# A hybrid mixer, mixture-of-experts and attention kernel on Trainium2: SBUF offsets of the second block's matmul operands set to fixed residues of 256 bytes

## Chip, cores and metric

One Trainium2 chip, one NeuronCore of it. The metric is the device time of one execution of the whole program, in microseconds (us). The input is one sequence of 256 tokens of width 1024, all in fp32.

## What is computed

The reference runs a first block (layer norm, a gated delta rule and a stick-breaking attention side by side, and a mixture of 32 experts) and on its result a second block. The change is meant for the second block; cut to what matters:

```
def second_block(x, ...):                       # x: 256 tokens of width 1024
    # layer 0
    x = x + moba_attention(rms_norm_2(x), w_qkv, w_o)        # 256 tokens: one causal block, 8 heads of 128
    x = x + squared_relu_mlp(rms_norm_2(x), w_up, w_down)    # 1024 -> 4096 -> 1024
    # layer 1
    x = x + pool_mixer(rms_norm_2(x), w_groups, ls_scale)    # trailing means, four groups of 256
    x = x + squared_relu_mlp(rms_norm_2(x), w_up, w_down)
    return rms_norm_2(x)

def squared_relu_mlp(x, w_up, w_down):
    h = jax.nn.relu(x @ w_up)
    return (h * h) @ w_down
```

In the first block each token goes to the two best experts of one group. The kernel gives each expert 32 places; an expert with more tokens gets a spare block of 32, whose expert is known only at run time.

## The kernel before

**Split products.** A dense product is done in fp32r, in three matmuls. Weights and activations are each split into a high part (a ScalarE cast, line 302) and a low part (a VectorE subtraction, line 303), and high x high, low x high and high x low are summed in PSUM. `Stream` loads weights in chunks of 1 MB (line 298), two *halves* to a chunk, and splits each half into one tile `wsplit` of 128 x 2048: the high part `wh` in the first 1024 columns, the low part `wl` in the rest.

**Two forms.** `ws_half` (lines 345 to 347) holds the weights stationary and lets 256 tokens move: 24 matmuls of 256 columns for a half. `xs_half` (358 to 360) and `down` inside `mlp` (1635 to 1637) hold the activations stationary and let the weights move: 12 matmuls of 512 columns for a half. Each matmul is preceded by the load of its stationary operand (LDWEIGHTS, engine PEld in the profile), which overlaps the matmul ahead of it.

**Stages of the second block.** Its 81 chunks are, in halves: 24 of q, k and v (`xs_half`), 8 of the attention's output (`ws_half`), 64 of the first feed-forward (32 halves up by `ws_half`, 32 down by `down`), 2 of the pooling (lines 1739 to 1741, weights stationary), 64 of the second feed-forward. Steadily, four halves up alternate with four halves down.

**Where the operands lie.** The second block's split tiles come from two pools in turn, `cvt` and `cvt2`, two tiles each; the pool changes after every two halves, shifted by one:

```
pool, tag = self.extra.get(self.i - 1) or (cvp[self.i // 2 % len(cvp)], "cv")
w = pool.tile([128, 2048], F32R, tag=tag, name="wsplit")
```

so that of four halves in a row the first and the fourth lie in one pool and the two between in the other. In the built program the tiles of `cvt` begin on a multiple of 256 bytes of a partition, those of `cvt2`, some 110 KB further on, 96 bytes past one (called *offset 0* and *offset 96* below; only the remainder by 256 is meant). The activations begin at offset 0 (`xh`, `xl`), 64 (`mhh`, `mhl`, the squared ReLU's two parts) or 96 (`oh`, `ol` of the attention; `ph`, `plo` of the pooling). Rows inside these tiles are multiples of 256 bytes apart. The offsets 64 and 96 come from small tiles that are allocated ahead: `r2` (8 bytes), `rss` (16), `rst`.

**Order.** A scheduler puts each engine's instructions in order when the program is built. In the experts' stage DVE (VectorE) does, besides its share of the products, two small chains. The *rotation* (lines 1164 to 1189, tiles `pos`, `ang`, `ki`, `kf`) makes angles for the second block's attention. *Who is next* (`who_is_next`, lines 1198 to 1209, tiles `xact`, `xjk`, `xwho`, `xwhoi`) finds the expert of the first spare block; SP reads `xwhoi` into registers (`where`, lines 1213 and 1214) to issue the three loads of that expert's weights (`spare_weights`, line 1219), and behind those, in SP's order, stand the other loads of experts' weights (line 922). `spare_tokens` (1230 to 1245) gathers the block's tokens (`xG`, `xGc`).

Of the kernel before, what the change touches and what calls it, by code (L numbers as in the profile page):

```python
# [10 lines left out]
F32 = mybir.dt.float32  # L11
F32R = mybir.dt.float32r
I32 = mybir.dt.int32
# [42 lines left out]
# --------------------------------------------------------------------------  # L56
# constants that depend on shapes alone, packed by column
# --------------------------------------------------------------------------
# [53 lines left out]
def _pool_matrix():  # L112
    """the trailing mean less the token itself, by window: [t', 144 of the first t | 128 of the last t]"""
    t = np.arange(SEQ)
    m = np.zeros((128, 4, 272), np.float32)
    for g, w in enumerate(WINDOWS):
        cnt = np.minimum(t + 1, w).astype(np.float32)
        inside = (t[:, None] <= t[None, :]) & (t[:, None] > t[None, :] - w)
        f = np.where(inside, np.float32(1.0) / cnt[None, :], 0.0) - np.eye(SEQ)
        m[:, g, :144] = f[:128, :144]  # L120
        m[:, g, 144:] = f[128:, 128:]
    return np.ascontiguousarray(m.reshape(128, 1088))


# order of the half chunks of the first stream of weights
# [3 lines left out]
def _fill_order():  # L129
    """dense work that fills the gaps of the recurrent mixers"""  # L130
    o = []
    sb = [[("sb", 3 * j + i) for i in range(3)] for j in range(4)]
    zs = [("z", i) for i in range(4)]
    g = [("g", m) for m in range(8, 16)] + [("g", m) for m in range(LATE, 8)]
    for c in FILL_SPEC:
        o += sb[int(c)] if c in "0123" else [zs.pop(0)] if c == "z" else [g.pop(0)]
    o += zs + g
    return o
# [4 lines left out]
             + [("o", i) for i in range(8)])  # L143

# [112 lines left out]
# --------------------------------------------------------------------------  # L257
# the kernel
# --------------------------------------------------------------------------
# [3 lines left out]
def tile_hybrid_block(ctx: ExitStack, tc: tile.TileContext, A, out, dump=None, stop=99):  # L263
# [41 lines left out]
    class Stream:  # L305
        """a dense part's weights in the order of their use, each split into two parts of 12 bits"""

        def __init__(self, dram, n_chunks, g_halves=(), extra={}):
            self.g_halves, self.extra, self.depth = g_halves, extra, 2
            self.dram, self.i, self.n, self.raw, self.q, self.got = dram, 0, n_chunks, [], [], 0  # L310
# [6 lines left out]
        def split(self):  # L317
            i, q = divmod(self.i, 2)
            self.i += 1
            if q == 0:  # L320
                self.load(i + N_RING)
                self.cur = self.raw.pop(0)
            s = slice(q * 1024, q * 1024 + 1024)
            pool, tag = self.extra.get(self.i - 1) or (cvp[self.i // 2 % len(cvp)], "cv")
            w = pool.tile([128, 2048], F32R, tag=tag, name="wsplit")
            wh, wl = w[:, :1024], w[:, 1024:]
            split_into(wh, wl, self.cur[:, s], G if self.i - 1 in self.g_halves else V)
            self.q.append((wh, wl))
# [9 lines left out]
    def ws_half(stream, m0, nk, xh, xl, width, fn, newbank):  # L338
        """out[m, t] for the m tiles of half a chunk: weights stationary, tokens moving; fn(m, psum)"""
        wh, wl = stream.half()  # L340
        for q in range(8 // nk):
            p = newbank()
            for k in range(nk):
                o = (q * nk + k) * 128
                PE.matmul(p[:, :width], wh[:, o:o + 128], xh[:, k, :], start=k == 0, stop=False)  # L345
                PE.matmul(p[:, :width], wl[:, o:o + 128], xh[:, k, :], start=False, stop=False)  # L346
                PE.matmul(p[:, :width], wh[:, o:o + 128], xl[:, k, :], start=False, stop=k == nk - 1)  # L347
            fn(m0 + q, p)

    def xs_half(stream, k0, nk, xh, xl, banks, t0=0):  # L350
        """out[t, 512] over two k tiles: tokens stationary, weights moving"""
# [10 lines left out]
    # 1 / sqrt(x): a first guess from the bits, two steps of rising order  # L362
# [21 lines left out]
    def rsqrt1(x):  # L384
        """of one column"""
# [13 lines left out]
    def moments(mv, s):  # L399
        """mean and variance of the rows, in one piece or two"""  # L400
# [8 lines left out]
    def ln_stats(s, eps=1e-5):  # L409
        """mean and 1 / deviation of the rows"""  # L410
# [27 lines left out]
    def warm(n):  # L438
        """matmuls whose result nobody wants: the tensor engine's clock stays up over a wait"""
# [34 lines left out]
    # rows of tokens, normalised; their gain and bias come with the transposing  # L474
# [20 lines left out]
    # a/b columns  # L495
# [4 lines left out]
    # delta-net channels: projection, causal convolution (of half weights: u), silu = u (1 + tanh u)  # L500
# [37 lines left out]
    def invert(At, n, levels, nm):  # L538
        """transposed inverse of I + A from A transposed, by doubling the size of the inverted blocks"""
# [35 lines left out]
    # the stick-breaking heads' work lies where the first of the experts' weights come  # L575
# [9 lines left out]
    def delta():  # L585
        # token scalars by head: beta, decay, exp(decay), exp(last decay - decay)
# [17 lines left out]
        # rows of k, their norms; back  # L604
# [86 lines left out]
        # what waits for q  # L691
# [18 lines left out]
        # and for v  # L710
# [22 lines left out]
        # states and outputs, chunk by chunk  # L733
# [14 lines left out]
        for c in range(2):  # L748
# [35 lines left out]
            # rms norm over the head, of the output scaled by q's norm  # L784
# [97 lines left out]
    def router_weights():  # L882
        """the router on rows less their mean: weights times the norm's gain less their mean; the bias's share"""
# [25 lines left out]
    def prefetch(n):  # L909
        """expert chunks on their way: up to n"""  # L910
# [58 lines left out]
    # first weights of the experts, while the dense part goes on  # L969
# [3 lines left out]
    # the delta-net's gates, its branch, merge; the gates' sigmoid is (1 + tanh) / 2  # L973
# [79 lines left out]
    # group: softmax, first maximum (of the probabilities: exp(d) is 1 from d = -2^-25 on)  # L1053
# [13 lines left out]
    # the two best experts of the group  # L1067
# [14 lines left out]
    # place of each token in the queue of its expert  # L1082
# [6 lines left out]
    def one_hot(g):  # L1089
        """[token, expert of four and place]"""  # L1090
# [7 lines left out]
    # weights of the two experts  # L1098
# [16 lines left out]
    # experts with more tokens than places: further blocks of CAP tokens, numbered over the experts  # L1115
# [21 lines left out]
    prefetch(n_slots)  # L1137

    def gather(g, Gt):
        """the tokens of four experts, transposed; the norm's gain and bias on the way"""  # L1140
# [13 lines left out]
    # the first gathering goes on between the first products  # L1154
# [5 lines left out]
    # rotation: angles reduced to [-pi, pi]  # L1160
# [17 lines left out]
    ki = moe.tile([128, 32], I32, name="ki")  # L1178
    kf = moe.tile([128, 32], F32, name="kf")
# [15 lines left out]
    def who_is_next():  # L1195
        """the expert whose block has the number in ctr, its group and place there (0, 0 and no tokens past the last)"""
        act = rt([32], "xact")
# [5 lines left out]
        jk = rt([32], "xjk")  # L1203
# [17 lines left out]
    def spare_tokens(act, off):  # L1221
        """the block's tokens, transposed, and its combining rows"""
# [4 lines left out]
        jk = rt([32], "xjk")  # L1227
# [22 lines left out]
    def spare_block(xx, pm, weights):  # L1250
        """an expert's output for the block; weights(i): two k tiles of gate and up, then two of down by half"""
# [36 lines left out]
    # the first of these blocks goes with the rest, any more in a loop  # L1288
# [24 lines left out]
    for g in range(NG):  # L1313
# [71 lines left out]
        if g == NG - 2:  # L1385
            # the residual's rows, with the first norm's gain and bias: they join the sums of the experts' outputs
# [26 lines left out]
    post = ctx.enter_context(tc.tile_pool(name="post", bufs=1, reuse_waits="tile"))  # L1413
    cvp.append(ctx.enter_context(tc.tile_pool(name="cvt2", bufs=2, reuse_waits="tile")))
    wpost = Stream(A["wpost"], 81, G_POST)

    def scaled(x, k, gname, xh, xl):
        """a k tile times the norm's gain, in two parts"""
# [21 lines left out]
    def mean_square(x, m, acc):  # L1440
        """sums of squares of the k tiles m - 1 and m, over those before"""
# [11 lines left out]
    def total(acc):  # L1453
        """one tile of sums from two of two"""
# [6 lines left out]
    def rstd(s):  # L1461
        """of sums of squares by token along the partitions: [128, 2]"""
# [11 lines left out]
    def to_rows():  # L1474
        """x with the tokens along the partitions"""
# [115 lines left out]
    def residual(gname, xh, xl, acc):  # L1591
        """adds a product to the residual; the next norm's operand and sum of squares follow"""
# [19 lines left out]
    def mlp(xh, xl, acc, n_last, after):  # L1612
# [3 lines left out]
        r2 = post.tile([128, 2], F32, tag="r2", name="r2")  # L1616
# [22 lines left out]
        def scale():  # L1639
            """1 / mean square, by token along the partitions"""  # L1640
# [34 lines left out]
    def rstd_rows(c, ss):  # L1675
        """of the rows' mean squares by half"""
        t = post.tile([128, 1], F32, tag="rst", name="rst")
# [10 lines left out]
    ss = post.tile([128, 2, 2], F32, tag="rss", name="rss")  # L1688
# [61 lines left out]
    ss = post.tile([128, 2, 2], F32, tag="rss", name="rss")  # L1750
# [38 lines left out]
```

## Time and profile before

| | us |
|---|---|
| runs: median of 3 (lowest, highest) | 1030.16 (1026.87, 1032.97) |
| the profiled execution: span from first to last instruction | 1031.7 |
| PE (matmul) busy | 957.0 |
| DVE, ACT busy | 588.1, 444.6 |

The profiled execution's own time outside its span is not given; the span is 1.5 us above the median of the runs and inside their range. PE is TensorE's matmuls, PEld its weight loads, DVE VectorE, ACT ScalarE, POOL GpSimd, SPq the DMA issues of SyncE. A matmul's duration holds its passage through the array, so matmuls that follow each other overlap in the rows: what one costs in a dense stretch is the distance from its start to the next one's start. The windows of single halves below have their edges at the start of the first matmul of each half, as the timeline shows these starts.

### The profile page before, as it was taken

To read this page: it belongs to the slowest core of one execution; us is meant where nothing else is said; L and a number is where in the kernel's file an instruction comes from. 1 tells how busy PE (TensorE), PEld (TensorE's weight loads), DVE (VectorE), ACT (ScalarE), POOL (GpSimd) and SP (SyncE) were. 2 spreads that over 40 slices of the span, in tenths; PEclk is the share of its full clock that TensorE was granted. 3 is DMA by queue.
4 is the path that set the end of the run, shared out by engine and by line. 5 is a ranking of instruction groups with operands and counts; after the bars stand their busy time and mean duration, and the time that the engine had idled before them with its cause. 6 is when DMAs were issued, how large, how long until landed. Compare 5 with 4: busy or idle time off the path is not lost.

```text
span 1031.7 us, 15809 instructions
## 1 busy us (share of the span) xinstructions
PE 957.0 (93%) x6369; PEld 778.3 (75%) x6369; DVE 588.1 (57%) x1131; ACT 444.6 (43%) x774; POOL 104.8 (10%) x75
## 2 busy tenths in 40 slices
PE   4889999999999988869979999999999999999996
PEld 3788988899884523324358889989999789999885
DVE  8887657584763211102276777655555586555554
ACT  3554655454432111102065565544444564444442
POOL 5343333000300000000040001000000020000001
PEclk9889999999999999989999999999999999999998
DMA  9222212749779999989956435455555525555521
GB/s 369 105 98 87 102 44 83 264 160 355 302 307 390 415 426 422 426 362 426 382 185 222 164 123 186 164 186 182 185 182 186 182 87 200 186 182 179 190 82 41
DMA packets 34234, 227.37 MB, mean 220 GB/s; under 512 B 3936, under 2 KB 4704, under 8 KB 7664
## 3 DMA queue, kind: packets, MB, share of 16 engines
q1 hardware_dynamic: 34160, 226.36, 57.8%
q8 instruction: 50, 0.82, 0.3%
q14 instruction: 24, 0.20, 0.1%
HBM read 225.29 MB, written 1.05 MB: 219 GB/s over the span
## 4 chain that ended last, share of the span: by engine, by line
PE 74%; DVE 10%; DMA 7%; ACT 4%; POOL 2%; issue 2%; SPq 0%; ACTq 0%; POOLq 0%; DVEq 0%
PE bank L347 10%; PE bank L346 9%; PE bank L345 9%; DMA wexp<-in_wexp_dram 6%; PE acc L1635 6%; PE acc L1636 6%; PE acc L1637 6%; PE bank L1335 5%; PE bank L359 3%; PE bank L360 2%; PE bank L358 2%; PE bank L1376 2%; PE acc L1303 2%; PE bank L1147 2%; DMA wraw<-in_wpre_dram 2%; DVE wsplit L303 2%
## 5 line engine op out<-in xcount | busy, mean ns | idle before, releaser
L303 DVE TENSOR_TENSOR wsplit<-wraw,wsplit 128x1024 fp32r<-128x1024 f32 x212 | 269.0, 1269 | 159.8 <-ACT wsplit L302 158.0
L302 ACT CAST wsplit<-wraw 128x1024 fp32r<-128x1024 f32 x222 | 231.7, 1045 | 152.5 <-PE acc L1637 94.9
L347 PE MATMUL bank<-xl,wsplit 128*128 128x256 f32 x512 | 144.3, 282 | 3.4 <-DVE xl L1420 3.4
L346 PE MATMUL bank<-xh,wsplit 128*128 128x256 f32 x512 | 143.9, 281 | 0.0
L345 PE MATMUL bank<-xh,wsplit 128*128 128x256 f32 x512 | 143.7, 281 | 0.0
L1635 PE MATMUL acc<-wsplit,mhh 128*128 128x512 f32 x256 | 101.7, 398 | 0.0
L1636 PE MATMUL acc<-wsplit,mhh 128*128 128x512 f32 x256 | 101.2, 395 | 0.0
L1637 PE MATMUL acc<-wsplit,mhl 128*128 128x512 f32 x256 | 101.1, 395 | 0.0
L347 PEld LDWEIGHTS bank<-xl,wsplit 128*128 128x128 f32 x512 | 97.2, 190 | 4.2 <-DVE xl L1420 4.2
L345 PE MATMUL bank<-hh,wsplit 128*128 128x256 f32 (+1 forms) x320 | 97.1, 303 | 1.6 <-DVE rcb L891 1.5
L347 PE MATMUL bank<-hl,wsplit 128*128 128x256 f32 (+1 forms) x320 | 94.3, 297 | 4.2 <-DVE hl L303 4.2
L345 PEld LDWEIGHTS bank<-xh,wsplit 128*128 128x128 f32 x512 | 97.1, 190 | 0.6
L346 PEld LDWEIGHTS bank<-xh,wsplit 128*128 128x128 f32 x512 | 97.0, 190 | 0.5
L346 PE MATMUL bank<-hh,wsplit 128*128 128x256 f32 (+1 forms) x320 | 94.8, 296 | 0.0
L1335 PE MATMUL bank<-wexp,xt 128*32 128x512 f32 x512 | 65.0, 622 | 7.4 <-DMA wexp<-in_wexp_dram 7.4
L347 PEld LDWEIGHTS bank<-hl,wsplit 128*128 128x128 f32 x320 | 63.4, 199 | 5.1 <-DVE hl L303 5.1
L345 PEld LDWEIGHTS bank<-hh,wsplit 128*128 128x128 f32 x320 | 64.0, 200 | 2.6 <-DVE rcb L891 1.7
L346 PEld LDWEIGHTS bank<-hh,wsplit 128*128 128x128 f32 x320 | 63.9, 200 | 0.3 <-issue 0.2
L1625 ACT ACTIVATE relu<-bank 128x256 f32<-128x256 f32 x64 | 24.7, 385 | 87.1 <-PE bank L347 87.1
L1637 PEld LDWEIGHTS acc<-wsplit,mhl 128*128 128x128 f32 x256 | 48.0, 188 | 11.5
L1636 PEld LDWEIGHTS acc<-wsplit,mhh 128*128 128x128 f32 x256 | 48.1, 188 | 11.2 <-DVE wsplit L303 0.3
L1635 PEld LDWEIGHTS acc<-wsplit,mhh 128*128 128x128 f32 x256 | 48.1, 188 | 11.0
(506 smaller groups left out, 1633.4 us busy)
## 6 DMA issues: line engine op xcount, KB each, us to landing
wexp<-in_wexp_dram SPq DMA_DIRECT2D x99, 1024.0 KB, 19.2
wraw<-in_wpost_dram SPq DMA_DIRECT2D x81, 1024.0 KB, 4.7
wraw<-in_wpre_dram SPq DMA_DIRECT2D x30, 1024.0 KB, 4.8
h<-in_x_dram SPq DMA_DIRECT2D x2, 512.0 KB, 4.1
eb<-in_rowv_dram SPq DMA_DIRECT2D x2, 512.0 KB, 10.1
out_dram<-of SPq DMA_DIRECT2D x4, 256.0 KB, 2.2
cpre<-in_cst_dram SPq DMA_DIRECT2D x1, 915.5 KB, 10.3
pmat<-in_poolm_dram SPq DMA_DIRECT2D x1, 544.0 KB, 4.5
```

The lines of the kernel that those rows point to most:

```text
L302: S.copy(hi, src)
L303: (sub or V).tensor_tensor(lo, src, hi.bitcast(F32), op=OP.subtract)
L345: PE.matmul(p[:, :width], wh[:, o:o + 128], xh[:, k, :], start=k == 0, stop=False)
L346: PE.matmul(p[:, :width], wl[:, o:o + 128], xh[:, k, :], start=False, stop=False)
L347: PE.matmul(p[:, :width], wh[:, o:o + 128], xl[:, k, :], start=False, stop=k == nk - 1)
L358: PE.matmul(banks[c], xh[:, k, tsl], w1, start=k == 0, stop=False)
L359: PE.matmul(banks[c], xh[:, k, tsl], w2, start=False, stop=False)
L1335: PE.matmul(pg[32 * e:32 * e + 32, :], xt[:, k, 32 * e:32 * e + 32], w[:, e, :], start=k == 0, stop=k == 7)
L1625: S.activation(t, p[:, :SEQ], AF.Relu)
L1635: PE.matmul(ac[c][n], hh_, wh, start=g == 0 and k == 0, stop=False)
L1636: PE.matmul(ac[c][n], hh_, wl, start=False, stop=False)
L1637: PE.matmul(ac[c][n], hl_, wh, start=False, stop=g == 7 and k == 3)
```

## The change

Besides dropping comments, docstrings and blank lines, it does three things.

```
+UP = [j < 2 or (j < 30 and (j - 2) % 4 < 2) for j in range(32)]
+STILL = [False] * 24 + [True] * 8 + [u for u in UP for _ in range(2)] + [True] * 2 + [u for u in UP for _ in range(2)]
+SHIFT = 24
...
-        def __init__(self, dram, n_chunks, g_halves=(), extra={}):
-            self.g_halves, self.extra, self.depth = g_halves, extra, 2
+        def __init__(self, dram, n_chunks, g_halves=(), extra={}, still=()):
+            self.g_halves, self.extra, self.depth, self.still = g_halves, extra, 2, still
...
-            w = pool.tile([128, 2048], F32R, tag=tag, name="wsplit")
-            wh, wl = w[:, :1024], w[:, 1024:]
+            if self.still:
+                o = SHIFT if self.still[self.i - 1] else 0
+                w = pool.tile([128, 2048 + 64], F32R, tag=tag, name="wsplit")
+                wh, wl = w[:, o:o + 1024], w[:, o + 1024:o + 2048]
+            else:
+                w = pool.tile([128, 2048], F32R, tag=tag, name="wsplit")
+                wh, wl = w[:, :1024], w[:, 1024:]
...
-    wpost = Stream(A["wpost"], 81, G_POST)
+    wpost = Stream(A["wpost"], 81, G_POST, still=STILL)
```

`STILL` says of each of the second block's 162 halves whether its weights are stationary. If so, its two parts begin 24 floats (96 bytes) into a tile that is 256 bytes longer. The first block's stream is as it was.

```
-        r2 = post.tile([128, 2], F32, tag="r2", name="r2")
+        r2 = post.tile([128, 64], F32, tag="r2", name="r2")[:, :2]
...
-        t = post.tile([128, 1], F32, tag="rst", name="rst")
+        t = post.tile([128, 64], F32, tag="rst", name="rst")[:, :1]
...
-    ss = post.tile([128, 2, 2], F32, tag="rss", name="rss")
+    ss = post.tile([128, 2, 32], F32, tag="rss", name="rss")[:, :, :2]
```

These small tiles now fill 256 bytes each. In the built program every `wsplit` tile and all of `xh`, `xl`, `mhh`, `mhl`, `oh`, `ol`, `ph`, `plo` begin at offset 0. So in the second block stationary weights lie at offset 96 against moving activations at 0, and moving weights at offset 0 against stationary activations at 0.

```
-    ki = moe.tile([128, 32], I32, name="ki")
-    kf = moe.tile([128, 32], F32, name="kf")
+    ki = moe.tile([128, 32], I32, tag="xjk", name="ki")
+    kf = moe.tile([128, 32], F32, tag="xact", name="kf")
...
-        act = rt([32], "xact")
+        act = rt([32], "xact", tag="xact")
...
-        jk = rt([32], "xjk")
+        jk = rt([32], "xjk", tag="xjk")
```

The rotation's `kf` and `ki` now share their memory with `xact` and `xjk`.

**What it moves.** ACT, POOL and SP keep their order; DVE and PE change at one place, in the experts' stage. On DVE, before, who is next and both `xG` stand right after the counting of blocks (`xsv` is of the same helper, `G` and `hid` belong to the experts):

```order
L1198 TENSOR_SCALAR xact<-cx,ctr 128x32
L1201 TENSOR_SCALAR xoff<-cx,ctr 128x32
L1199 SCALAR_TENSOR_TENSOR xact<-ci,ctr,xact 128x32
...
L1209 CAST xwhoi<-xwho 1x2
L1230 SCALAR_TENSOR_TENSOR xjk,xs_3548<-xact,xsv 128x32
L1231 SCALAR_TENSOR_TENSOR xjk,xs_3548<-xact,cmb 128x32
L1232 TENSOR_SCALAR xG<-cst,xs_3548 128x32
...
L1051 TENSOR_TENSOR G<-cst,rk 128x256
L1361 TENSOR_TENSOR hid<-hid,bank 128x256
```

In the changed kernel (its line numbers are 10 higher) they stand behind the whole rotation, whose last rows are the two of `ang`:

```order
L1197 TENSOR_TENSOR ang<-ang,kf 128x32
L1199 TENSOR_SCALAR ang<-ang 128x64
L1208 TENSOR_SCALAR xact<-cx,ctr 128x32
L1209 SCALAR_TENSOR_TENSOR xact<-ci,ctr,xact 128x32
L1216 SCALAR_TENSOR_TENSOR xjk,xwho<-xact,cst 128x32
L1284 TENSOR_SCALAR ctr<-ctr 128x1
L1216 SCALAR_TENSOR_TENSOR xjk,xwho<-xact,cst 128x32
L1219 CAST xwhoi<-xwho 1x2
...
L1242 TENSOR_SCALAR xG<-cst,xs_3548 128x32
...
L1391 COPY ys<-bank 128x256
L1242 TENSOR_SCALAR xG<-cst,xs_3548 128x32
```

So all of the rotation, and the experts' `G`, `hid`, `xt`, `hT` and `ys` rows that stood between the two chains, now come ahead of `xwhoi`. On PE, at the same place, before and then in the changed kernel:

```order
L1376 MATMUL bank<-wexp,hT 32x512 x12
L1237 MATMUL bank<-xG,h_77 128x32 x3
L1376 MATMUL bank<-wexp,hT 32x512 x4
L1237 MATMUL bank<-xG,h_77 128x32 x13
L1245 MATMUL bank<-cst,xGc 32x128 x2
```

```order
L1386 MATMUL bank<-wexp,hT 32x512 x12
L1247 MATMUL bank<-xG,h_77 128x32
L1255 MATMUL bank<-cst,xGc 32x128
L1386 MATMUL bank<-wexp,hT 32x512 x4
L1247 MATMUL bank<-xG,h_77 128x32 x15
L1255 MATMUL bank<-cst,xGc 32x128
```

One transpose of `xGc` moved ahead of an expert's four matmuls and two gathering matmuls moved behind them; the rest is in the order of before.

## Rows read from the trace of the kernel before

**Rows 1.** The page: busy time by engine, and the last chain's shares by engine.

```profile
PE 957.0 (93%) x6369; PEld 778.3 (75%) x6369; DVE 588.1 (57%) x1131; ACT 444.6 (43%) x774; POOL 104.8 (10%) x75
...
PE 74%; DVE 10%; DMA 7%; ACT 4%; POOL 2%; issue 2%; SPq 0%; ACTq 0%; POOLq 0%; DVEq 0%
```

**Rows 2.** Windows by stage: length, then busy of PE, PEld, DVE, ACT, POOL; clock, DMA, GB/s.

```profile
309.00:345.00 36.00, 34.12 (x274) 16.24 (x270) 14.68 (x70) 8.29 (x18) 0.00 (x0) 1.00 0.96 392
345.00:509.00 164.00, 140.99 (x890) 57.73 (x890) 26.22 (x64) 18.56 (x47) 0.00 (x0) 0.97 0.98 408
520.00:1032.00 512.00, 492.75 (x3089) 441.06 (x3088) 326.10 (x556) 260.34 (x426) 25.26 (x18) 0.99 0.47 162
```

**Rows 3.** Waits of PE in the second block: total, times, longest.

```profile
PE bank L1430 <- DVE r L396: 3.7, 1, 3.7
PE bank L347 <- DVE xl L1420: 3.4, 4, 1.3
```

**Rows 4.** Windows of single halves, PE only: four up, then two down.

```profile
673.49:676.37 2.88, 2.88 (x26) 1.00 0.35 148
676.37:679.18 2.81, 2.81 (x26) 1.00 0.75 236
679.18:682.00 2.82, 2.82 (x26) 1.00 0.34 142
682.00:684.87 2.87, 2.87 (x26) 1.00 0.60 188
...
690.92:693.72 2.80, 2.80 (x13) 1.00 0.32 135
693.72:696.51 2.79, 2.79 (x13) 1.00 0.72 235
```

**Rows 5.** The same for two halves of the attention's output, split tiles of `cvt2`.

```profile
629.20:632.08 2.88, 2.88 (x27) 1.00 0.79 242
632.08:634.95 2.87, 2.87 (x26) 1.00 0.30 123
```

**Rows 6.** The same for halves of q, k, v: tiles of `cvt` thrice, then of `cvt2`.

```profile
553.88:556.60 2.72, 2.72 (x14) 1.00 0.01 3
...
563.08:565.84 2.76, 2.76 (x13) 1.00 0.90 306
565.84:568.56 2.72, 2.72 (x13) 1.00 0.18 75
568.56:571.37 2.81, 2.81 (x13) 1.00 0.40 87
```

**Rows 7.** Groups by line in 673.49 to 696.51: DVE's and ACT's share of a split.

```profile
L303 DVE TENSOR_TENSOR wsplit<-wraw,wsplit 128x1024 fp32r<-128x1024 f32 x8 | 9.8, 1226 | 8.1 <-ACT wsplit L302 8.1
...
L302 ACT CAST wsplit<-wraw 128x1024 fp32r<-128x1024 f32 x8 | 8.4, 1045 | 6.3 <-PE acc L1637 6.3
```

**Rows 8.** Timeline of DVE around who is next and the rotation's end: start, duration.

```profile
312.56 0.23 DVE L1198 TENSOR_SCALAR xact<-cx,ctr 128x32 f32<-128x32 f32 x1
...
313.67 0.16 DVE L1209 CAST xwhoi<-xwho 1x2 int32<-1x2 f32 x1
...
342.68 0.20 DVE L1189 TENSOR_SCALAR ang<-ang 128x64 f32<-128x64 f32 x1
```

**Rows 9.** SP's read of `xwhoi`: duration ns least, median, most; first and last start.

```profile
L1213 SPq TENSOR_LOAD <-xwhoi x1: 483/483/483, 329.0 to 329.0; - x1
```

**Rows 10.** Timeline of SP's loads: start, time from first to last, count.

```profile
328.61 0.33 SPq L922 DMA_DIRECT2D wexp<-in_wexp_dram  x1
331.16 14.37 SPq L1219 DMA_DIRECT2D wexp<-in_wexp_dram  x3
345.63 6.07 SPq L922 DMA_DIRECT2D wexp<-in_wexp_dram  x6
```

**Rows 11.** Line 922's load of 328.6: us from issue to landing.

```profile
DMA to landing us min/median/max: 20.1/20.1/20.1
```

**Rows 12.** A window as in rows 2.

```profile
346.00:351.00 5.00, 5.00 (x39) 3.71 (x32) 1.50 (x4) 0.37 (x1) 0.00 (x0) 1.00 1.03 390
```

More of the change, by code (lines that the diff above doesn't have):

```diff
@@ L1226, in spare_tokens @@
         s1 = rt([2, 2], "xs1")
-        jk = rt([32], "xjk")
+        jk = rt([32], "xjk", tag="xjk")
         for c in range(2):
@@ L1749, in tile_hybrid_block @@
     nf = row("norm_final", act1, "rowsA")
-    ss = post.tile([128, 2, 2], F32, tag="rss", name="rss")
+    ss = post.tile([128, 2, 32], F32, tag="rss", name="rss")[:, :, :2]
     fin = ctx.enter_context(tc.tile_pool(name="fin", bufs=1, reuse_waits="tile"))
```

## The prediction

> **What bounds the kernel now.** I read the page first: PE is busy for 957 of 1031.7 us and holds 74% of the last chain [rows 1]. That is a mean over stages, so the windows by stage come next [rows 2]. From 309 to 509 us the DMA engines are busy for 96 to 98% of the time: there the loads of the experts' weights set the end. From 520 us to the end, the second block, DMA is at 47%, DVE at 326 of 512 us, and PE at 493 of 512. PE's waits there are few, the two largest 3.7 and 3.4 us in all [rows 3]. So in the second block a shorter matmul is a shorter kernel, as long as nothing behind PE becomes late.
>
> A matmul's price can't be read from its duration, since neighbours overlap; it is read from the length of a half in which PE never stops. Four halves up in a row take 2.88, 2.81, 2.82 and 2.87 us [rows 4]. They do the same work on the same activations, at a granted clock of 1.00 in each. What differs is the pool: the first and the fourth have weights at offset 0, the two between at 96, and the activations are at 0. DMA load doesn't sort them: of the slow ones one has a DMA share of 0.35 and one of 0.60, of the fast ones one 0.75 and one 0.34. So (weights 0, activations 0) costs 2.875 and (96, 0) 2.815 us.
>
> That it is the pair of offsets, and not the pool, the attention's output says: there the weights lie in the pool that was fast above, but the activations are at 96 too, and the halves take 2.88 and 2.87 us [rows 5].
>
> With the weights moving, q, k and v tell the pools apart the other way round: weights at 0 against stationary activations at 0 take 2.72 to 2.76 us, weights at 96 take 2.81 [rows 6]. The halves down take 2.80 and 2.79 in one pool and in the other [rows 4]: there the stationary activations are at 64 in both.
>
> **The change, part by part.** It adds no instruction to the second block and removes none; it moves every half to the better pair of its form.
>
> *Up, 64 halves.* 32 of them are at (0, 0) and go to (96, 0): 32 x (2.875 - 2.815) = 1.9 us.
>
> *Down, 64 halves.* They go from stationary 64, moving 0 or 96, to 0 and 0. No half down shows that pair, but q, k and v have the same form and shape. Their steady value is 2.72; 2.76 stands directly behind other work. I take 2.73, near the steady value since all halves down will be alike: 64 x (2.795 - 2.73) = 4.2 us. The bounds: 64 x (2.795 - 2.76) = 2.2 us and 64 x (2.795 - 2.72) = 4.8 us; if the pair is not the cause here, nothing.
>
> *q, k, v, 24 halves.* 12 have their weights at 96: 12 x (2.81 - 2.73) = 0.9 us, between 0.4 (if half of it vanishes in the interruptions by the attention's heads) and 1.1.
>
> *Attention's output, 8 halves,* from (0, 96) or (96, 96) to (96, 0): 8 x (2.875 - 2.815) = 0.5 us. *Pooling, 2 halves,* of the same form: 0.1 us.
>
> *What hides the splits.* ACT takes 1.05 us and DVE then 1.23 us to split a half [rows 7], 2.28 us in a row if nothing overlaps. A half down will take 2.73, so the split stays hidden, with some 0.4 us to spare. Half of the splits in these rows already write to offset 96, the tiles of `cvt2`, so writing there can't be much dearer. The longer tiles and the small tiles of 256 bytes cost space and no time.
>
> *The experts' stage.* Here something gets later. `kf` now owns the memory of `xact`, so who is next can start only when the rotation is through. Before, it ran from 312.56 to 313.83, 1.27 us; the rotation ended at 342.88 [rows 8]. So `xwhoi` is ready at 342.88 + 1.27 = 344.15. SP read it at 329.0 [rows 9] without waiting and issued the first spare load 2.16 us later [rows 10]. Now SP stands still for 15.1 us, and the load goes out at 344.15 + 2.16 = 346.3 instead of 331.2. Behind it in SP's order stand the other two spare loads and all later loads of experts' weights. In a stage bounded by DMA that could cost up to 15.1 us. What covers it is the queue: the load ahead, issued at 328.6, needed 20.1 us to land [rows 11], at 348.7, because those ahead of it came first. At 392 to 408 GB/s [rows 2] a load of 1 MB takes about 2.6 us, so the engines still have more than 2 us of work when the first spare load comes. The third spare load was held until 345.6 anyway [rows 10], so that line 922 goes on at about 348 instead of 345.6, and behind it the order is as before. The window from 346 to 351 with its DMA share of 1.03 [rows 12] stays full. I count 0; the bounds are 0 and 2 us, the latter if a new load needs that long to get the engines going. On PE the one transpose that moved waits for `xGc` some tenths of a us, in a stage where PE waits for weights later.
>
> **Sum.** 1.9 + 4.2 + 0.9 + 0.5 + 0.1 = 7.6 us less, all in the second block. Against the profiled span: 1031.7 - 7.6 = 1024.1. The median of the runs shown is 1.5 us below that span, so for the median: 1030.2 - 7.6 = 1022.6 us.
>
> **Rivals.**
> 1. *Halves down don't care.* Their activations come fresh from ACT and DVE and their sums alternate between four banks; if that sets 2.80 and not the 64, only the rest remains: 1.9 + 0.9 + 0.5 + 0.1 = 3.4, so 1026.8 us. For it: no row shows a half down at another offset. Against it: 2.80 is also what q, k, v cost at a bad pair [rows 6], and at 64 the pool makes no difference, as if one bad operand were enough.
> 2. *Offsets decide nothing.* The two pools also lie some 110 KB apart in a partition, and the place could be what a read feels; the change leaves the places and the turns of the pools as they are, so the halves stay as they are: 1030.2 us. Against it: the same pool is fast in rows 4 and slow in rows 5. The Trainium skill speaks for this rival: by "TensorE: Matmul & The Clock Gate", section "Step-by-step: what each phase is for", TensorE has two independent read ports to SBUF, and loading the next weights takes nothing from the running matmul, so where the two operands lie would not matter and the time would be that of before. The trace disagrees: 2.88 against 2.81 us for equal halves [rows 4].
> 3. *Slower: SP's wait reaches the DMA engines.* The place is line 1213. If the queue's 20 us do not cover it (the spare loads come in small pieces, and three at once behind an empty queue may start slowly), the stall enters in full: 1030.2 + 15.1 - 7.6 = 1037.7 us. It begins to cost when the first spare load leaves later than about 346.5, and each us beyond that costs one; the gain is eaten at 354. For it: SP stands behind one word. Against it: 328.6 + 20.1 is later than 346.3 [rows 10, 11].
>
> **How the numbers follow.** A measurement of this kernel can tell about 0.5% from no change, 5.2 us. My forecast has a chance of 0.71, the first rival 0.14, the second 0.09, the third 0.06. The forecast's own bounds: at least 1.9 + 2.2 + 0.4 + 0.5 = 5.0 us, at most 1.9 + 4.8 + 1.1 + 0.6 = 8.4, so 1021.8 to 1025.2; the runs' scatter of 3 us to either side of their median adds to it. The range reaches over the first rival, from 1019.5 to 1027.2. Faster by over 0.5%: the forecast but for its lowest end, 0.67. Within 0.5%: that end and the first two rivals, 0.27. Slower: the third, 0.06.
>
> **What would show it right or wrong.** Halves up all 2.81 to 2.82 us, halves down 2.72 to 2.76, the attention's output 2.82, q, k, v 2.72 to 2.76, each at a clock of 1.00. The matmuls' mean durations hardly move; the distances between their starts do. SP's read of `xwhoi` starts late or lasts to about 344, the first spare load leaves near 346, and the DMA share from 346 to 351 stays at 1. The second block should begin where it did. I am wrong if halves down stay at 2.80, if halves of one form still come in two lengths, if new waits of PE for `wsplit` appear, or if the stage of the experts ends later.

## The result, and the profile after

The changed kernel took 1025.93 us in the median of 22 runs (1019.52 to 1029.30), the kernel before, run beside it, 1031.11 (1026.87 to 1034.81). The ratio is 0.9943, with an interval of 0.9928 to 0.9958: by the ratio 5.9 us less, between 4.3 and 7.4. The forecast was 1022.6, 7.6 less than a median of 1030.16. The profiled run took 1027.14 us, 2.3 of them outside its span of 1024.8.

The page of the changed kernel, busy time and the last chain's shares, beside [rows 1]:

```profile
PE 945.8 (92%) x6369; PEld 773.4 (75%) x6369; DVE 589.4 (58%) x1131; ACT 444.5 (43%) x774; POOL 104.5 (10%) x75
...
PE 77%; DVE 12%; ACT 4%; POOL 2%; DMA 2%; issue 2%; SPq 0%; ACTq 0%; POOLq 0%; DVEq 0%
```

PE is busy for 11.2 us less with the same number of matmuls, and no other engine's time moved by more than 5. Windows of single halves, columns as in [rows 4 to 6]; first four halves up and two down, then two of the attention's output, then three of q, k, v:

```profile
672.34:675.15 2.81, 2.81 (x25) 1.00 0.46 192
675.15:677.97 2.82, 2.82 (x26) 1.00 0.76 221
677.97:680.78 2.81, 2.81 (x26) 1.00 0.36 152
680.78:683.60 2.82, 2.82 (x26) 1.00 0.61 186
686.79:689.51 2.72, 2.72 (x14) 1.00 0.80 241
689.51:692.23 2.72, 2.72 (x14) 1.00 0.35 145
617.41:620.22 2.81, 2.81 (x26) 1.00 0.00 0
620.22:623.04 2.82, 2.82 (x26) 1.00 0.00 0
563.26:565.98 2.72, 2.72 (x13) 1.00 0.87 280
565.98:568.70 2.72, 2.72 (x13) 1.00 0.25 105
568.70:571.43 2.73, 2.73 (x14) 1.00 0.43 90
```

In this profile every form now has one length, apart from halves beside a wait or other work, where before it had two or more: up 2.81 to 2.82, down 2.72, q, k, v 2.72 to 2.73. The second block's two largest waits of PE are those of [rows 3], so nothing took the place of what went:

```profile
PE bank L1440 <- DVE r L406: 3.7, 1, 3.7
PE bank L357 <- DVE xl L1430: 3.4, 4, 1.3
```

The experts' stage is the other half of the story. DVE's timeline: the rotation's last instruction, then the cast into `xwhoi`, beside [rows 8] (start, duration):

```profile
341.92 0.20 DVE L1199 TENSOR_SCALAR ang<-ang 128x64 f32<-128x64 f32 x1
...
343.05 0.16 DVE L1219 CAST xwhoi<-xwho 1x2 int32<-1x2 f32 x1
```

SP's read of `xwhoi` (beside [rows 9]), then SP's issues (beside [rows 10]), then how long the three spare loads took to land (beside [rows 11]):

```profile
L1223 SPq TENSOR_LOAD <-xwhoi x1: 470/470/470, 343.2 to 343.2; - x1
```

```profile
344.95 2.07 SPq L1229 DMA_DIRECT2D wexp<-in_wexp_dram  x3
347.12 1.98 SPq L932 DMA_DIRECT2D wexp<-in_wexp_dram  x1
```

```profile
DMA to landing us min/median/max: 7.8/9.5/11.4
```

Windows of 1 us around it (length, clock, DMA share, GB/s), where [rows 12] had 1.03 and 390:

```profile
346.00:347.00 1.00, 1.00 0.69 125
347.00:348.00 1.00, 1.00 0.94 350
348.00:349.00 1.00, 1.00 1.03 391
```

The first spare load left at 344.95, 1.4 us earlier than forecast. All the same the engines ran dry: 125 GB/s for one us where they had moved 390.

For all runs I took the same few moments from the traces' records: when the load ahead of the first spare load landed, when that spare load was issued and landed, how long from the load ahead to the last of the experts' loads, and how long the second block took from the start of its fourth half to the end of the last instruction that an engine computes. (us; zero is the first such instruction, 0.3 us off the profile's zero.)

```
run            ahead    spare    spare    landed   to last  second
               landed   issued   landed   apart    load     block
before         348.44   330.91   351.06   2.62     160.0    490.9
after          347.00   344.69   352.47   5.47     162.9    483.0
again          346.76   343.62   349.53   2.77     160.8    483.2
offsets_only   339.61   321.91   342.23   2.62     160.3    483.1
move_only      338.89   336.27   341.91   3.02     161.4    489.9
sweep_weights  347.72   344.87   350.55   2.82     161.2    488.3
sweep_acts     348.10   344.44   352.08   3.98     162.7    488.7
sweep_fine     349.93   346.25   353.07   3.14     162.1    484.8
all_at_64      344.56   327.04   347.20   2.64     160.0    482.5
no_padding     348.33   330.96   350.97   2.64     160.1    487.8
kick_scan      342.63   325.25   345.26   2.63     159.9    478.1
at_224         339.07   321.58   341.69   2.62     160.2    481.5
kick_rows      346.54   329.15   349.18   2.64     160.4    480.9
kick_at_96     348.08   330.34   350.72   2.64     160.2    484.3
```

In the changed kernel the second block is 7.9 us shorter and the experts' stage 2.9 longer. The difference of the spans, 6.9, is these two, 1.4 us that the stages ahead happened to be faster, and 0.5 between the last load and the second block.

### The profile page after: what moved, and what is told of

It is laid out like the page before. It is cut to its first block, busy times and chain, and to the rows that moved or that the text cites. A ratio compares the mean times of both kernels' runs of the same rounds, so it can differ in the third digit from the quotient of the medians.

```text
span 1024.8 us, 15811 instructions
## 1 busy us (share of the span) xinstructions
PE 945.8 (92%) x6369; PEld 773.4 (75%) x6369; DVE 589.4 (58%) x1131; ACT 444.5 (43%) x774; POOL 104.5 (10%) x75
## 4 chain that ended last, share of the span: by engine, by line
PE 77%; DVE 12%; ACT 4%; POOL 2%; DMA 2%; issue 2%; SPq 0%; ACTq 0%; POOLq 0%; DVEq 0%
PE bank L357 10%; PE bank L356 9%; PE bank L355 9%; PE bank L1345 6%; PE acc L1645 5%; PE acc L1646 5%; PE acc L1647 5%; PE bank L1157 3%; PE bank L1386 3%; PE acc L1313 3%; PE bank L369 2%; PE bank L370 2%; PE bank L368 2%; DMA wexp<-in_wexp_dram 2%; DVE wsplit L308 2%
## 5 line engine op out<-in xcount | busy, mean ns | idle before, releaser
L1645 PE MATMUL acc<-wsplit,mhh 128*128 128x512 f32 x256 | 100.4, 393 | 0.0
L1646 PE MATMUL acc<-wsplit,mhh 128*128 128x512 f32 x256 | 99.8, 390 | 0.0
L1647 PEld LDWEIGHTS acc<-wsplit,mhl 128*128 128x128 f32 x256 | 48.1, 188 | 10.1
```

Source lines behind the costliest of these rows:

```text
L1645: PE.matmul(ac[c][n], hh_, wh, start=g == 0 and k == 0, stop=False)
L1646: PE.matmul(ac[c][n], hh_, wl, start=False, stop=False)
L1647: PE.matmul(ac[c][n], hl_, wh, start=False, stop=g == 7 and k == 3)
```

## Experiments

### The same kernel again, and the two halves of the change apart

`again` is the changed kernel. `offsets_only` keeps its offsets and shares `kf` and `ki` with tiles of the spare block that are written later, so that every engine has the order of before (the sharing saves room in SBUF; no run shows how much would be lacking without it). `move_only` is the kernel before with the change's sharing alone.

```
 offsets_only, against the changed kernel
-    ki = moe.tile([128, 32], I32, tag="xjk", name="ki")
-    kf = moe.tile([128, 32], F32, tag="xact", name="kf")
+    ki = moe.tile([128, 32], I32, tag="xhT", name="ki")
+    kf = moe.tile([128, 32], F32, tag="xx", name="kf")
...
-        act = rt([32], "xact", tag="xact")
+        act = rt([32], "xact")
...
-        xx = rt([8, CAP], "xx")
+        xx = rt([8, CAP], "xx", tag="xx")
```

> The changed kernel once more, beside the next two. First theory: the offsets take some 7.3 us from the second block and the moved who-is-next gives 1.5 to 3 us back in the experts' stage, in sum 0.994 of the kernel before. Rival: the offsets take 5.9 us and the move nothing: the same 0.994. This run only sets the mark for the other two on the same chip.

> The offsets as in the changed kernel, but ki and kf share memory with xhT and xx instead of xjk and xact, which brings every engine back to the order of before. First theory: SP reads xwhoi without waiting, the landing of the first spare load follows the one ahead after 2.5 us instead of 5.5, and the kernel is 1.5 to 3 us faster than the changed one: about 7.3 us less than before, a ratio of 0.993 or a little under. Rival: the same time as the changed kernel, 0.994 to 0.9945, since the stage waits elsewhere anyway.

> The kernel before with only the shared memory of ki and kf, no offset changed. First theory: SP waits at line 1213 to about 344, the first spare load lands 5.5 us behind the one ahead, and the kernel is 1.5 to 3 us slower than before: 1.0015 to 1.003. Rival: the queue covers it and the time is that of before, 1.000.

Measured: `again` 0.9925 (0.9902 to 0.9948), `offsets_only` 0.9911 (0.9890 to 0.9932), `move_only` 1.0005 (0.9980 to 1.0029). By time alone `again` and `offsets_only` can't be told apart; the traces can. The offsets are worth 7.8 us in the second block (490.9 to 483.1) with no instruction moved. The moved who is next gains nothing and costs 0.8, 1.4 and 2.9 us in the experts' stage in three traces, for one and the same order; the time of `move_only` alone, between 2.1 us less and 3.0 more than before, is too coarse to show such a cost. So the offsets are the whole gain, and this way of sharing is a price that the change need not have paid.

### Which offsets matter, and to whom

`sweep_weights` gives the split weights 0, 32, ... 224 bytes in turn, two halves each, counted apart for the two forms; `sweep_fine` does so in steps of 16 where they are stationary and leaves 0 where they move; `sweep_acts` leaves the weights at 0 and moves the activations of down, 32 bytes further with each group.

```
-                o = SHIFT if self.still[self.i - 1] else 0
+                o = self.offset(self.i - 1)
...
+        def offset(self, i):
+            same = [j for j in range(i) if self.still[j] == self.still[i]]
+            return 8 * (len(same) // 2 % 8)
```

```
+            oa = 8 * g
+            hh_ = post.tile([128, 4 * SEQ + 64], F32R, tag="mh", name="mhh", bufs=2)[:, oa:oa + 4 * SEQ].rearrange("p (m t) -> p m t", t=SEQ)
```

> The changed kernel with the split weights' offset stepped through 0, 32, 64 ... 224 bytes, two halves each, apart for halves whose weights are stationary and whose weights move; activations stay at 0. Read is the length of each half. First theory, the pair decides: with stationary weights 2.88 us at 0 and 2.82 at 96, and some other offsets that are as good; with moving weights 2.72 at 0 and 2.80 or more at most others. Rival, place or pool decides: all halves of a form alike, or two lengths that follow the pools' turns and not the offset.

> The changed kernel with the squared ReLU's parts, stationary in the halves down, moved to 0, 32, 64 ... 224 bytes, one offset for each group of four halves; the weights stay at 0. First theory, the pair of offsets decides: 2.72 us a half at 0, about 2.80 at 64 as before the change, most others 2.79 to 2.81. Rival (halves down do not care about their stationary operand; the gain came from the weights that no longer lie at 96): 2.72 at every offset.

> The changed kernel with stationary weights at 0, 16, 32 ... 240 bytes, two halves each, activations and moving weights at 0. The coarse sweep gave halves up of 2.88 at 0 and 160, 2.84 at 32, 2.82 at 96 and 192 and, at 64, 2.83 in the first feed-forward but 2.72 to 2.74 in the second. First theory, offset alone: each offset has one length, the same in both feed-forwards, and 64 was disturbed by its neighbours of other offsets; a smooth course between the points of the coarse sweep. Rival, a second condition (the bank of PSUM, or how the two reads fall in step): 48 to 80 again have two lengths, by feed-forward.

Each was executed once (1031.93, 1033.33 and 1029.66 us), for the lengths of the halves. Halves down in `sweep_acts`, weights at 0, stationary activations at 0, 32 and 192:

```profile
669.52:672.24 2.72, 2.72 (x13) 1.00 0.35 145
692.26:695.06 2.80, 2.80 (x14) 1.00 0.30 126
803.34:806.09 2.75, 2.75 (x14) 1.00 0.63 179
```

Lengths by offset, worked out from the starts in the traces (us; a dash where only halves beside a wait lay there, a plus where the shortest of four stands and the longest took 0.02 to 0.04 more):

```
bytes past a multiple of 256       0     32    64    96    128   160   192   224
down, weights move, acts at 0      2.72  2.80  2.75  2.80  2.79  2.81  2.80  2.80
down, acts move,  weights at 0     2.72  2.80  2.80  2.81  2.80  2.80  2.75  2.80
up, first feed-forward (fine)      2.88  2.84  -     2.85  2.88  2.88  2.83  2.80
up, second feed-forward (fine)     2.87  2.84  2.83  2.82  2.88  2.88  2.83  2.80
up, second feed-forward (steps 32) 2.88  2.84  2.72+ 2.82  2.85+ 2.88  2.83  2.80+
```

For down the answer is plain: both operands on a multiple of 256 is the one pair that gives 2.72, and moving either of them costs 0.03 to 0.09 us. For up the picture has a flaw: at 64, with the same remainders, the table holds 2.83 and 2.72. `sweep_acts` shows the same at 96, where all its halves up lie. A half of the group behind halves down with activations at 0, then one of the group behind halves down with activations at 32:

```profile
677.78:680.60 2.82, 2.82 (x27) 1.00 0.70 232
700.70:703.55 2.85, 2.85 (x26) 1.00 0.78 230
```

Behind halves down at 0, 64, 128 and 160 the halves up took 2.82 us, behind those at 32 and 96 they took 2.85, in both feed-forwards alike.

### 64 instead of 96, and the small tiles as they were

`all_at_64` is `offsets_only` with SHIFT = 16. `no_padding` is `offsets_only` with `r2`, `rst` and `rss` as small as before, so that down's activations lie at 64 and the attention's at 96 again, and the second pool's weights at 96 more than the first's.

```
-SHIFT = 24
+SHIFT = 16
```

```
-        r2 = post.tile([128, 64], F32, tag="r2", name="r2")[:, :2]
+        r2 = post.tile([128, 2], F32, tag="r2", name="r2")
```

> The offsets of the changed kernel but stationary weights at 64 instead of 96, and the order of before (ki and kf share with xhT and xx). If 64 by itself is the cheapest, as in the second feed-forward of the sweep: halves up of 2.72 us, 74 x 0.095 = 7 us less than the same with 96, a ratio of 0.984 to 0.985. If only the second feed-forward gains: half of that, 0.988. If the short halves were an effect of mixed offsets: 2.83, that is 1 us more than with 96, 0.992.

> The shift of stationary weights stays, the order is that of before, but r2, rst and rss are as small as they were: activations go back to 64 and 96, the second pool back to 96, so that half of the moving weights lie at 96 and half of the stationary ones at 192. First theory: halves up 2.82 at 96 and 2.83 at 192; halves down 2.79 to 2.81 as before the change, q, k, v of the second pool 2.81; in sum some 5.5 us more than with the padding, a ratio of 0.997. Rival (halves down do not care): 0.993.

`no_padding` gave 0.9977 (0.9949 to 1.0004): down back at 2.79 to 2.80 us, a second block of 487.8. So some 4.7 of the 7.8 us hang on the small tiles, the part of the diff that looks like a trifle. `all_at_64` gave 0.9925 (0.9893 to 0.9958), and a puzzle. Three of its halves up, the first before any half down, the others behind halves down:

```profile
649.68:652.40 2.72, 2.72 (x26) 1.00 0.59 244
666.50:669.32 2.82, 2.82 (x25) 1.00 0.43 180
669.32:672.15 2.83, 2.83 (x27) 1.00 0.74 243
```

In both feed-forwards eight halves up stand ahead of the first down; the last six of them, which ran without a wait, took 2.72, and all that came behind halves down 2.83, although the four tiles in turn have the very same addresses in both. So neither remainder nor place can be all; what ran just before is the likely difference.

### A small matmul between a half down and a half up

`kick_scan` puts one small matmul of the same operands, overwritten by the next, ahead of each group of four halves up that follows halves down, with another width in each of the 12 groups.

```
+            if kick:
+                PE.matmul(p[:, :kick], wh[:, :128], xh[:, 0, :kick], start=True, stop=True)
             for k in range(nk):
```

> The kernel with stationary weights at offset 64 and the order of before, with one small matmul more ahead of each group of four halves up that follows halves down (12 groups; its columns 16, 32, 64, 96, 128, 192 in the first feed-forward and 48, 80, 112, 160, 224, 256 in the second). Without it, halves up at the very same addresses took 2.72 us in the first six of a feed-forward and 2.827 in all that follow halves down. Theory A (two rhythms): loads and matmuls settle into one of two steps to each other, and stay in it until something disturbs them; then some widths of the small matmul bring the four halves behind it to 2.72 us and others leave them at 2.827, four alike each time. Theory B (the company decides: once halves down run between, the sums, splits and ReLUs of ACT and DVE that run beside the halves up are others): all 48 halves stay at 2.827, whatever the width. The time is one look: by A, with half of the widths good, some 2.5 us less than the 1021.3 of that kernel, and 12 small matmuls of some 0.1 us more, so about 1020; by B about 1022.5.

One execution, 1015.25 us (before: 1029.55, median of 11); what it is read for is the lengths inside it. A group with a small matmul of 16 columns in front, all four halves, then two halves of the last group, whose small matmul has 256 columns:

```profile
664.23:667.08 2.85, 2.85 (x26) 1.00 0.47 195
667.08:669.80 2.72, 2.72 (x26) 1.00 0.69 235
669.80:672.52 2.72, 2.72 (x26) 1.00 0.37 151
672.52:675.25 2.73, 2.73 (x27) 1.00 0.56 168
...
974.08:976.90 2.82, 2.82 (x26) 1.00 0.02 6
976.90:979.73 2.83, 2.83 (x26) 1.00 0.00 0
```

Eleven widths of twelve, from 16 to 224 columns, bring the halves to 2.72, the first with the small matmul's own time on top; only 256, which is one more matmul of the usual width, leaves them at 2.83. The small matmul costs 0.13 to 0.15 us and gains four times 0.107. The second block is 4.4 us shorter than in `all_at_64`. That the company of other engines decides (theory B) is out: nothing was changed there, and 44 of the 48 halves changed their length.

### Two more versions, and the kick at 96

`at_224` has the halves up at 224 and the attention's output and pooling at 64. `kick_rows` has 64 everywhere and uses, for four of the six groups, the transposes of the residual's rows as the disturbance, by calling `next(rows)` ahead of `up(g + 1)`; the other two groups get a small matmul. `kick_at_96` is `offsets_only` with a small matmul of 96 columns in all 12 groups.

```
-SHIFT = 24
+SHIFT = [16 if 24 <= i < 32 or 96 <= i < 98 else 56 for i in range(162)]
```

```
+            if 0 < g < 5:
+                t = next(rows)
             if g < 7:
                 up(g + 1)
             if g == 0:
                 scale()
-            if 0 < g < 5:
-                t = next(rows)
```

> The order of before, activations at offset 0, weights at 0 where moving; stationary weights at 224 in the halves up (2.80 us in the finest sweep, in both feed-forwards) and at 64 in the attention's output and the pooling (2.72 to 2.83 us where they lay there). Against the kernel with 96 everywhere, whose halves up took 2.815: 64 x 0.015 = 1.0 us, six of them that took 2.847 another 0.3, and the attention's output 7 x 0.127 = 0.9: 2.2 us less. Expected, if a length goes with its offset: halves up 2.80, the second block about 481 us, ratio to the kernel before about 0.989. If the length depends on the rhythm that was carried in from the half before: some halves up above 2.82 although all lie at 224, ratio 0.991 or more.

> Stationary weights at offset 64, the order of before in the experts' stage. Of each feed-forward's six groups of halves up that follow halves down, four now come directly behind the four transposes of the residual's rows (which stood ahead of the next halves down until now), and the last two behind a small matmul of 96 columns. Theory A (two rhythms, 2.72 and 2.827 us for a half up at the same addresses, kept until something comes between): any other matmul between a half down and a half up puts the rhythm right, the transposes too. Then all halves up take 2.72: 12 groups x 4 x 0.107 = 5.1 us less than with 64 and no kick, 4 small matmuls cost 4 x 0.12 = 0.5, and 8 halves down that no longer follow transposes save 0.1 each: 5.4 us less, a second block of 477 instead of 482.5 us, a ratio to the kernel before of about 0.987. Rival (only a matmul of the same operands puts it right): the 8 groups behind transposes stay at 2.827 us, 1.2 us less at most, ratio 0.991.

> The order of before, stationary weights at offset 96 as in the change, and a small matmul of 96 columns more ahead of each of the 12 groups of halves up that follow halves down. Without it, halves up at 96 took 2.847 us in the first six of the second feed-forward, and 2.815 behind halves down. Theory A (each offset has two rhythms, and what came just before chooses): the small matmul sends the 48 halves up behind it to the other rhythm, 2.847: here the kick is a loss of 48 x 0.03 = 1.4 us and 12 x 0.12 = 1.4 more for itself, a second block of 483.1 + 2.9 = 486. Rival (the kick just clears something, and any half up behind it is faster): 2.72 to 2.80 us, a second block of 481 or less.

`at_224`: 0.9916 (0.9889 to 0.9943), its second block 481.5. Halves up behind halves down took 2.80 as expected, but the first six of each feed-forward 2.83: this offset too has two lengths, the other way round from 64.

`kick_rows`: 0.9874 (0.9840 to 0.9907), the best ratio measured with an interval; the second block took 480.9, not 477. Three halves of the first group behind transposes, then three of the third:

```profile
670.36:673.18 2.82, 2.82 (x27) 1.00 0.30 122
673.18:675.90 2.72, 2.72 (x26) 1.00 0.83 268
675.90:678.62 2.72, 2.72 (x26) 1.00 0.28 117
714.87:717.78 2.91, 2.91 (x27) 1.00 0.27 110
717.78:720.61 2.83, 2.83 (x27) 1.00 0.94 313
720.61:723.43 2.82, 2.82 (x26) 1.00 0.15 61
```

Six of the eight groups behind transposes went to 2.72, the third of each feed-forward stayed at 2.83, and this time the attention's output and the first six halves up ran at 2.83 as well, at the addresses at which they had taken 2.72 in `all_at_64`. Those 19 halves and two groups make up 2.9 of the 3.9 us that were missed, the eight first halves behind transposes, 2.82 to 2.91 long, another 0.8.

`kick_at_96`: one execution, 1027.21 us. The halves behind the kick kept their 2.815:

```profile
671.59:674.51 2.92, 2.92 (x26) 1.00 0.41 174
674.51:677.33 2.82, 2.82 (x26) 1.00 0.81 256
677.33:680.15 2.82, 2.82 (x27) 1.00 0.29 122
```

The kick cost its own 0.11 us twelve times (484.3 against 483.1) and did nothing else. Both expectations fell: it neither sent the halves to 2.847 nor made them faster. Two lengths do exist at 96, but this kick doesn't choose between them.

Nor does the program alone choose. `again` is the changed kernel, instruction for instruction and address for address; a half of its attention's output, then one of the first six of the second feed-forward that run without a wait:

```profile
615.69:618.54 2.85, 2.85 (x26) 1.00 0.00 0
843.08:845.93 2.85, 2.85 (x27) 1.00 0.90 279
```

In the profile of `after` the attention's output took 2.81 to 2.82, as shown above, and the half of the second feed-forward 2.82:

```profile
844.52:847.34 2.82, 2.82 (x26) 1.00 0.90 291
```

So which of two lengths comes differs between executions of one kernel, and a length seen in a single profile, as in `kick_scan` and `kick_at_96`, can differ in the next.

## Why the prediction was right, and where it was off

**The bound.** Right: the second block is bounded by PE, and shorter halves made it shorter with the same waits.

**The terms.** Summed from each matmul's start to the next one's start, the halves down went from 180.0 to 175.7 us: 4.3 where 4.2 was forecast, 0.07 to 0.08 for most halves and less for the first of each group. The halves up went from 186.8 to 184.8: 1.9, as forecast. q, k and v gained 0.6 where 0.9 was forecast, the attention's output 0.5, the pooling nothing. That makes 7.3 of the 7.6; POOL's sum, for which PE waited 1.0 us before and 0.4 now, brings most of the rest of the 7.9.

That up came out as forecast is in part luck. The prices 2.875 and 2.815 were read in the first feed-forward [rows 4]. Four halves up in a row of the second, in the kernel before:

```profile
874.28:877.13 2.85, 2.85 (x26) 1.00 0.40 167
877.13:879.99 2.86, 2.86 (x26) 1.00 0.78 238
879.99:882.87 2.88, 2.88 (x26) 1.00 0.31 131
882.87:885.69 2.82, 2.82 (x26) 1.00 0.72 209
```

Here the pools' turns are the other way round, so the first and the fourth have weights at 96 and the two between at 0: the pair (96, 0) took 2.85 and 2.82 us in one kernel, and the trace of before already showed it. And in `again`, the same kernel, up gained 1.7, since six halves of the second feed-forward took 2.85.

**The experts' stage: the step that failed.** "I count 0" was wrong, and "the engines still have more than 2 us of work when the first spare load comes" was right but not enough. The forecast had that load leave 2.4 us ahead of the landing before it; it left 2.3 ahead of it. A load that meets a queue running dry took 5.6 to 7.8 us from issue to landing (`after` 7.8, `again` 5.9, `move_only` 5.6), so a lead of 2.3 to 3.7 us leaves a hole. In the profile of the change the two landings lay 2.9 us further apart than in the kernel before, over the upper bound of 2, in the five others with this order 0.1 to 1.4; up to the last load the stage lost 0.8 to 2.9 us. The lead alone doesn't sort them, and what else decides stays open. These losses have the size of what lacks between the 7.6 us forecast and the 5.9 measured, but the times are too coarse to show that they are the reason: `again`, the same kernel with a loss of 0.8 in its trace, measured 7.7, between 5.4 and 10.1. Rival 3 had the right place but the wrong price: the hole did not grow with the 15 us that SP stood still, since the queue covered nearly all of them.

**Rival 1** (halves down don't care) fell with `after` and `sweep_acts`. **Rival 2** (offsets decide nothing) fell too, with `offsets_only` against before and within one kernel in `sweep_acts`. The Trainium skill was called to speak for it ("TensorE: Matmul & The Clock Gate", section "Step-by-step: what each phase is for": two independent read ports, so that loading weights takes nothing from the running matmul). What the prediction drew from that, that the operands' place would not matter, does not hold in these runs: halves of equal work took 2.72, 2.75 and 2.80 us as one operand's offset went through 0, 192 and 32. Whether the loads take anything from the matmuls no run shows.

**The tale behind the pairs** was too simple, though the sum suffered little. I took a pair of remainders to have one length. For down that held within some 0.03 us in every kernel; for up at 64, 96 and 224 the same addresses had two lengths. Which came went with what PE had run before (`sweep_acts`, `kick_scan`), but not with that alone, as `after` and `again` show. Why an offset matters, and what the two lengths are inside TensorE, no run shows.

## What to carry to other kernels

Where PE never stops, read the length of equal pieces of work from start to start, sorted by where their operands lie in SBUF: here 2 to 3% of a half's time lay in byte offsets, and fixing them took small tiles padded to 256 bytes and one shift. If one piece has two lengths at equal addresses, try a tiny matmul ahead of it; here 16 columns bought 0.3 us per group in one profile, at one offset and not at another. And take more than one profile of a kernel before a length is called that of an offset. When a pool is too tight for a change like this, let the tiles share memory with something that is written later: sharing with a producer that a load's address hangs on put a hole of up to 2.9 us into a stage that DMA bounds.

## What was not expected of the hardware

Besides the two lengths at one address: TensorE's clock early in the program differs between executions of kernels that are alike there. Windows from 30 to 50 us (length, PE busy, clock, DMA share, GB/s), first of the changed kernel's profile:

```profile
30.00:40.00 10.00, 8.53 (x51) 0.71 0.10 20
40.00:50.00 10.00, 10.00 (x81) 1.00 0.32 115
```

then of `offsets_only`:

```profile
30.00:40.00 10.00, 10.00 (x82) 1.00 0.30 105
40.00:50.00 10.00, 5.73 (x45) 1.00 0.50 178
```

In the first the granted clock fell to 0.71 in the mean, so part of that stretch ran at 1.2 GHz; in the 10 us ahead PE had been busy for 5.26 us there and for 7.07 in `offsets_only`, where the clock stayed at 1.00. The stretch in which PE never stops and starts some 82 matmuls in 10 us begins 10 us later in the first. `move_only`, which has the order of `after`, was spared as well, so it isn't the change that decides. The load ahead of the first spare one landed at 339 us in these two and in `at_224`, and at 347 to 348 in before and after. This may be a part of why medians of a few runs wander: those of the kernel before, taken anew beside each set of experiments, went from 1029.37 to 1032.73; since of each set only the profiled executions have a trace, it is not shown.
